# Side work planned by the engines that its next steps use, and the first two weight groups loaded and split in parts, in a two-layer decoder step on one core

## The chip, the cores and the metric

One core of a Trainium2 chip runs the whole step. The metric is the device time of one execution in microseconds (us). Shown before the change are three runs: a median of 1090.82 us, from 1090.24 to 1092.0.

## What is computed

Two decoder layers over 288 token columns: a prompt of 256 tokens and 8 sequences of 4 new tokens, with D = 1024. Cut to what matters:

```python
g, u_pool, u_conf, u_sc, q, k, v, qi, ki, wi = split_cols(x @ w_in)
a = pool_mixer(u_pool)                       # windows of 2, 4, 8, 16
b = silu(layer_norm(dwconv31(ga * sigmoid(gb)) + conv_b))
c = sb * dwconv3(sc_ * sh)
d = attend(q, k, v, topk(index_scores(qi, ki, wi)))
merged = sum(sigmoid(g[i]) * (branch[i] @ w_br[i]) for i in range(4))
x1 = layer_norm(ALPHA * x + merged @ w_o)
r = ALPHA * x1 + (silu(x1 @ w_hg) * (x1 @ w_hu)) @ w_ffn_out
r = r + (pe @ w_pe) * sigmoid(r @ w_pg)
y = layer_norm(r)
```

## The kernel before

All activations lie feature-major: 128 features on the partitions, 288 token columns. Every weight matrix is cut into 128 x 128 tiles, and the host lays the 2448 tiles out in the order in which TensorE will use them, in 306 groups of G = 8. Each product is made from three fp32r matmuls on numbers split into a high and a low part: high weight by high input, high weight by low input, low weight by high input. One group therefore holds 24 matmuls.

A weight group passes through three engines before TensorE can use it. SyncE's queue loads it (`wraw`, 512 KB, L239), ScalarE makes the high part (`whi`, L245), and VectorE subtracts it from the raw weights to make the low part (`wlo`, L252). `fetch` (L231 to 254) does this ahead of use: when TensorE comes to group g, the load of group g + 5, the high part of g + 3 and the low part of g + 2 are issued. `W` (called for each tile) calls `fetch` and then `side` when a new group begins.

`side` (L200) sets the order of everything that isn't a big product: it is a planner that runs while the program is written. The side jobs are Python generators (`conv`, `pool`, `sconv`, `topk` within the indexers, the two attentions). Each step of a job issues a few instructions and yields their estimated cost as a pair, (VectorE us, ScalarE us). Each group begins one tick, in which each engine gets a budget (1.96 us of VectorE, 2.3 us of ScalarE); the tick takes steps only while **both** engines have budget left:

```python
        while min(self.left) > 0:
            ready = [t for t in self.tasks if t.wake <= self.tick]
            if not ready:
                break
            ready = [t for t in ready if not t.low] or ready
```

A step that yields a plain number sleeps that many ticks. `conv`, the causal depthwise convolution with 31 taps (62 VectorE instructions at L653 and L655 for the prompt columns, six more from L661 for the samples, then a LayerNorm, a SiLU and `parts`, which splits the result at L633 and L637), is the only job of low priority. Where the main program needs a job's result, `finish` runs what is left of it on the spot, with no big product between its steps. `layer` calls `finish(conv)` after the products of the attention branch and before those of the convolution branch (`w_br_conv`), whose inputs are what L633 and L637 write. In the order before the change, `conv` is not done at that point in either layer: 8 calls of its generator are left in the first, 3 in the second.

The program begins in `run`: three warming matmuls on zeros (L1209), the input x in five loads (chunks 0, 1, 2-3, 4-5, 6-7 of 8), the weight groups between them, group 0 in two halves. Six column tiles are then accumulated over the 8 chunks of x by `outer` (L293, L295, L297), 18 matmuls for each chunk, called part 0 to part 7 here. Part k needs chunk k of x, cast and subtracted on VectorE (L1220, L1221), and the weight tiles 6k to 6k + 5; group 0 covers part 0 and two tiles of part 1.

Of the kernel before, what the change touches and what calls it, by code (L numbers as in the profile page):

```python
# [105 lines left out]

class Task:
    def __init__(self, gen, low):
        self.gen, self.wake, self.done, self.low = gen, 0, False, low


class Builder:
# [74 lines left out]
    def step(self, t):  # L187
# [6 lines left out]
        if isinstance(r, int):  # L194
            t.wake = self.tick + r
        else:
            self.left[0] -= r[0]
            self.left[1] -= r[1]

    def side(self):  # L200
# [3 lines left out]
        while min(self.left) > 0:  # L204
            ready = [t for t in self.tasks if t.wake <= self.tick]
# [25 lines left out]
    def fetch(self, g, only=0):  # L231
# [4 lines left out]
        while self.ndma <= to[0]:  # L236
            t = self.wp.tile([128, G * 128], F32, name="wraw", tag="wraw", bufs=4)
            for c in cut(self.ndma):
                nc.sync.dma_start(t[:, c], self.d["w"][self.ndma][:, c])  # L239
            self.raw[self.ndma] = t  # L240
            self.ndma += 1
        while self.nhi <= to[1]:
            t = self.wp.tile([128, G * 128], F32R, name="whi", tag="whi", bufs=4)
            for c in cut(self.nhi):
                nc.scalar.activation(t[:, c], self.raw[self.nhi][:, c], AF.Copy)  # L245
            self.hi[self.nhi] = t
            self.nhi += 1
        while self.nlo <= to[2]:
            t = self.wp.tile([128, G * 128], F32R, name="wlo", tag="wlo", bufs=3)
            raw = self.raw.pop(self.nlo)  # L250
            for c in cut(self.nlo):
                nc.vector.tensor_tensor(t[:, c], raw[:, c], self.hi[self.nlo][:, c].bitcast(F32), op=OP.subtract)  # L252
            self.lo[self.nlo] = t
# [28 lines left out]
    def outer(self, name, cols, rh, rl, nk):  # L282
        outs = []

        def part(k):
# [3 lines left out]
            while n < len(cols):  # L289
                now = min(G - len(self.keys) % G, len(cols) - n) if k < nk - 1 else 1  # L290
# [3 lines left out]
                for o, wh, wl in w:  # L294
                    m(o, wl, rh[:, k], start=False, stop=False)  # L295
                for o, wh, wl in w:
                    m(o, wh, rl[:, k], start=False, stop=k == nk - 1)  # L297
# [279 lines left out]
    def pool(self):  # L577
        nc, pe = self.nc, self.pe
        s1 = yield from self.get_b([128, 2, PE_])
# [16 lines left out]
        for c in range(2):  # L596
            for r0, src in ((0, s1), (64, s2)):
# [10 lines left out]
                yield 0.65, 0  # L608
        self.free(3)
# [764 lines left out]
```

## Time and profile before

| what | value |
|---|---|
| median of 3 runs | 1090.82 us |
| the profiled execution, its own time | 1090.84 us |
| its span, first to last instruction | 1089.1 us |
| TensorE busy (matmul) | 1066.8 us, 98% |
| VectorE busy | 770.1 us, 71% |
| ScalarE busy | 560.7 us, 51% |
| GpSimd busy | 171.6 us, 16% |
| DMA, mean | 173 GB/s |
| mean granted TensorE clock | 0.994 |

The busy time of TensorE is a sum of modelled matmul spans that overlap, so it isn't read as the share of useful work. How many matmuls begin in a stretch says more: a group of 24 takes about 3.2 us when nothing holds it up. A row of the timeline gives the start, the length, the engine, the line, the tile written and the tiles read, and in brackets how long the engine had been idle and what ended that.

### The profile page before, as it was taken

What the parts mean: (1) busy time and instruction counts of PE and PEld (TensorE: products, weight loads), DVE (VectorE), ACT (ScalarE), POOL (GpSimd) and SP (SyncE); (2) the same over time, 40 slices, a digit from 0 to 9 for tenths busy, and PEclk for the clock granted to TensorE, in tenths of its full rate; (3) what the DMA queues carried; (4) which work ended last, traced back from release to release, by engine and by line L of the source; (5) the groups of instructions that cost most, each with busy time, mean ns of one, the idle gap of its engine ahead of it and who ended that gap; (6) DMA issues with size and microseconds to landing.
All of it is one profiled execution on the core that took longest, in us unless ns stands there. A gap on an engine that the chain in (4) does not pass through costs nothing.

```text
span 1089.1 us, 20628 instructions
## 1 busy us (share of the span) xinstructions
PE 1066.8 (98%) x8138; PEld 1030.1 (95%) x8138; DVE 770.1 (71%) x1302; ACT 560.7 (51%) x930; POOL 171.6 (16%) x175
## 2 busy tenths in 40 slices
PE   8999999999999999999999999999989999999996
PEld 7999989899999999999999999998989999999995
DVE  5896958579885565544789877776697856655456
ACT  4875445445564444433579564644535644444334
POOL 0730002004510000000527100030045000000004
PEclk9999999999999999999999999999989999999998
DMA  8576556644445455555445854565433654554541
GB/s 302 164 244 212 173 174 232 195 147 135 155 148 184 155 173 168 166 170 167 154 154 171 295 171 155 195 213 184 140 132 117 193 174 156 167 170 166 175 136 44
DMA packets 61299, 188.57 MB, mean 173 GB/s; under 512 B 7538, under 2 KB 11666, under 8 KB 61202
## 3 DMA queue, kind: packets, MB, share of 16 engines
q1 hardware_dynamic: 60210, 183.69, 51.7%
q0 software_dynamic: 992, 3.57, 0.9%
q8 instruction: 64, 1.05, 0.4%
q14 instruction: 33, 0.27, 0.1%
HBM read 182.48 MB, written 4.75 MB: 172 GB/s over the span
## 4 chain that ended last, share of the span: by engine, by line
PE 89%; DVE 5%; issue 2%; ACT 2%; POOL 2%; DMA 1%; SPq 0%; DVEq 0%; POOLq 0%
PE mm L271 24%; PE mm L272 24%; PE mm L273 23%; PE mm L295 2%; PE mm L297 2%; PE mm L293 2%; DVE wlo L252 2%; PE ax L272 1%; PE ax L273 1%; PE ax L271 1%; POOL b L317 1%; PE ax L295 1%; PE ax L297 1%; POOL b L348 1%; PE ax L953 1%
## 5 line engine op out<-in xcount | busy, mean ns | idle before, releaser
L252 DVE TENSOR_TENSOR wlo<-wraw,whi 128x1024 fp32r<-128x1024 f32 (+1 forms) x307 | 383.3, 1251 | 155.0 <-issue 83.8
L271 PE MATMUL mm<-xh,whi 128*128 128x288 f32 x1536 | 455.1, 296 | 0.0
L273 PE MATMUL mm<-xh,wlo 128*128 128x288 f32 x1536 | 453.1, 295 | 0.3 <-DVE wlo L252 0.3
L272 PE MATMUL mm<-xl,whi 128*128 128x288 f32 x1536 | 453.2, 295 | 0.0
L245 ACT ACTIVATE whi<-wraw 128x1024 fp32r<-128x1024 f32 (+1 forms) x307 | 322.6, 1052 | 148.1 <-PE mm L272 74.0
L271 PEld LDWEIGHTS mm<-xh,whi 128*128 128x128 f32 x1536 | 288.8, 188 | 8.1 <-issue 6.4
L273 PEld LDWEIGHTS mm<-xh,wlo 128*128 128x128 f32 x1536 | 288.6, 188 | 0.9 <-DVE wlo L252 0.9
L272 PEld LDWEIGHTS mm<-xl,whi 128*128 128x128 f32 x1536 | 288.8, 188 | 0.3
L271 PE MATMUL mm<-b,whi 128*128 128x288 f32 x576 | 171.0, 297 | 0.3 <-DVE s L1030 0.2
L272 PE MATMUL mm<-b,whi 128*128 128x288 f32 x576 | 169.9, 295 | 0.0
L273 PE MATMUL mm<-b,wlo 128*128 128x288 f32 x576 | 169.7, 295 | 0.0
L271 PEld LDWEIGHTS mm<-b,whi 128*128 128x128 f32 x576 | 108.3, 188 | 1.3 <-issue 0.4
L272 PEld LDWEIGHTS mm<-b,whi 128*128 128x128 f32 x576 | 108.3, 188 | 0.3
L273 PEld LDWEIGHTS mm<-b,wlo 128*128 128x128 f32 x576 | 108.2, 188 | 0.0
L1031 POOL TENSOR_TENSOR m<-m,s 128x288 f32<-128x288 f32 x32 | 35.3, 1129 | 274.6 <-DVE s L1030 274.6
L315 POOL TENSOR_TENSOR b<-xf 128x288 f32<-128x288 f32 x4 | 4.9, 1218 | 442.4 <-DVE xf L1176 433.5
L1149 ACT ACTIVATE b<-s 128x288 fp32r<-128x288 f32 x44 | 19.3, 446 | 92.4 <-DVE s L1144 92.4
L655 DVE SCALAR_TENSOR_TENSOR b<-b,prm 128x256 f32<-128x256 f32 x120 | 62.1, 569 | 0.0
L1144 DVE TENSOR_TENSOR s<-s,mm 128x288 f32<-128x288 f32 x40 | 18.0, 454 | 50.5 <-PE mm L273 50.5
L1015 ACT ACTIVATE g<-mm 128x288 f32<-128x288 f32 x32 | 13.2, 412 | 67.7 <-PE mm L273 67.7
L1015 ACT ACTIVATE xf<-mm 128x288 f32<-128x288 f32 x32 | 13.2, 411 | 51.1 <-PE mm L273 51.0
L1152 DVE TENSOR_TENSOR b<-s,b 128x288 fp32r<-128x288 f32 x44 | 19.8, 458 | 19.5 <-ACT b L1149 19.5
(254 smaller groups left out, 1243.7 us busy)
## 6 DMA issues: line engine op xcount, KB each, us to landing
wraw<-in_w_dram SPq DMA_DIRECT2D x305, 512.0 KB, 3.5
kv<-in_ck_dram SPq DMA_DIRECT2D x32, 256.0 KB, 5.0
kv<-in_cv_dram SPq DMA_DIRECT2D x32, 256.0 KB, 4.3
out_ko_dram<-b POOLq DMA_DIRECT2D x2, 576.0 KB, 4.7
out_vo_dram<-b POOLq DMA_DIRECT2D x2, 576.0 KB, 6.9
kv<-in_kidx_dram SPq DMA_DIRECT2D x32, 32.0 KB, 3.0
xf<-in_x_dram SPq DMA_DIRECT2D x3, 288.0 KB, 6.5
b<-in_p_dram SPq DMA_DIRECT2D x3, 288.0 KB, 4.0
```

The lines of the kernel that those rows point to most:

```text
L245: nc.scalar.activation(t[:, c], self.raw[self.nhi][:, c], AF.Copy)
L252: nc.vector.tensor_tensor(t[:, c], raw[:, c], self.hi[self.nlo][:, c].bitcast(F32), op=OP.subtract)
L271: m(out, wh, rh, start=first, stop=False)
L272: m(out, wh, rl, start=False, stop=False)
L273: m(out, wl, rh, start=False, stop=last)
L293: m(o, wh, rh[:, k], start=k == 0, stop=False)
L295: m(o, wl, rh[:, k], start=False, stop=False)
L297: m(o, wh, rl[:, k], start=False, stop=k == nk - 1)
L655: nc.vector.scalar_tensor_tensor(o, e, wj, o, op0=OP.mult, op1=OP.add)
L1015: self.nc.scalar.activation(g, a, AF.Sigmoid)
L1031: nc.gpsimd.tensor_tensor(self.m[:, j], self.m[:, j], t, op=OP.add)
L1152: nc.vector.tensor_tensor(h[:, 1, i % 2], t, h[:, 0, i % 2].bitcast(F32), op=OP.subtract)
```

## The change

**The planner.** A task says which engines its next steps use (`needs`): both, which is the default, or VectorE alone. A step may be taken when every engine it needs has budget left, so a task that needs VectorE alone goes on after ScalarE's budget of the tick is spent. `conv` (taps and samples), `pool` (window sums) and `topk` declare such stretches with `yield VECTOR` and end them with `yield BOTH`.

**The first weights.** Group 0 is loaded and split in three parts (2, 2 and 4 tiles), group 1 in two (4 and 4); `outer` takes tiles by these parts (`room`). For the first two groups the second batch of matmuls is the one on the low input and the third the one on the low weight; it was the other way round. Chunk 0 of x is loaded from ScalarE's queue, chunks 2 and 3 are loaded apart, and the loads, splits and products are written out in the order of use. The warming matmuls read a constant that GpSimd sets and no longer one that VectorE sets.

```diff
+VECTOR, BOTH = (0,), (0, 1)
...
+        elif r is VECTOR or r is BOTH:
+            t.needs = r
...
-        while min(self.left) > 0:
-            ready = [t for t in self.tasks if t.wake <= self.tick]
+        can = lambda t: not t.done and t.wake <= self.tick and all(self.left[i] > 0 for i in t.needs)
+        while True:
+            ready = [t for t in self.tasks if can(t)]
             if not ready:
                 break
             ready = [t for t in ready if not t.low] or ready
             for t in ready:
-                if not t.done and min(self.left) > 0:
+                if can(t):
                     self.step(t)
...
+    def load(self, i):
+        g, c = self.ndma, cut(self.ndma)
+        if i == 0:
+            self.raw[g] = self.wp.tile([128, G * 128], F32, name="wraw", tag="wraw", bufs=4)
+        self.nc.sync.dma_start(self.raw[g][:, c[i]], self.d["w"][g][:, c[i]])
+        self.ndma += i == len(c) - 1
...
-                now = min(G - len(self.keys) % G, len(cols) - n) if k < nk - 1 else 1
+                now = min(room(len(self.keys)), len(cols) - n) if k < nk - 1 else 1
+                early = len(self.keys) < 2 * G
...
+                for second in ((1, 0) if early else (0, 1)):
+                    for o, wh, wl in w:
+                        if second:
+                            m(o, wh, rl[:, k], start=False, stop=not early and k == nk - 1)
+                        else:
+                            m(o, wl, rh[:, k], start=False, stop=False)
...
         bias = self.par("conv_b")
         es = [ce[:, c, 30 + TP:].rearrange("p (b w) -> p b w", b=NB) for c in range(2)]
+        yield VECTOR
         for j in range(31):
...
             yield 0.1, 0
+        yield BOTH
         self.free()
...
-        zero = self.s()
-        nc.vector.memset(zero, 0.0)
+        zero = nc.const_aps.tensor(0.0, (128, N), F32)
...
+        ks = [slice(0, 1), slice(1, 2), slice(2, 3), slice(3, 4), slice(4, 6), slice(6, 8)]
+        move(ks[0], nc.scalar)
+        for i in range(3):
+            self.load(i)
+        move(ks[1], nc.sync)
+        self.load(0)
+        move(ks[2], nc.sync)
+        self.load(1)
+        self.load(0)
+        move(ks[3], nc.sync)
+        move(ks[4], nc.sync)
+        self.load(0)
+        move(ks[5], nc.sync)
...
+        parts(ks[0])
+        for i in range(3):
+            self.high(i)
+            if i == 2:
+                parts(ks[1])
+            self.low(i)
+        part(0)
+        self.high(0)
+        self.low(0)
+        part(1)
...
+EDGES = {0: (0, 2, 4, 8), 1: (0, 4, 8)}
...
+def room(n):
+
+    g, i = divmod(n, G)
+    return next(e for e in EDGES.get(g, (0, G)) if e > i) - i
```

`high(i)` and `low(i)` are made like `load(i)`: they issue the ScalarE copy and the VectorE subtraction of part i of the next group. `move` is a load of x from the queue named, `parts` the cast and the subtraction of a chunk of x.

VectorE, second layer, before the change, from the convolution's centring (L677) to the first product of its branch (L1104). L252 is the low part of one weight group, so one such row stands for one group; L304 splits the next layer input `p`, L691 to L706 are the convolution's LayerNorm and SiLU, L637 its split, L1030 the gating of the attention branch:

```order
L677 SCALAR_TENSOR_TENSOR b<-ax,b 128x288 x2
L252 TENSOR_TENSOR wlo<-wraw,whi 128x1024
L304 TENSOR_TENSOR b<-b 128x576
L252 TENSOR_TENSOR wlo<-wraw,whi 128x1024
L691 RECIPROCAL s<-s 128x288
...
L696 TENSOR_TENSOR b<-b,s 128x288 x2
...
L706 TENSOR_TENSOR b<-b,s 128x288 x2
L1030 TENSOR_TENSOR s<-mm,g 128x288 x2
L637 TENSOR_TENSOR b<-b 128x288 x2
L252 TENSOR_TENSOR wlo<-wraw,whi 128x1024
L1104 TENSOR_TENSOR ax<-ax,xf 128x288
```

The same place with the change (L705 was L677, L271 was L252, L719 to L734 were L691 to L706, L328 was L304, L663 was L637, L1060 was L1030, L1134 was L1104):

```order
L705 SCALAR_TENSOR_TENSOR b<-ax,b 128x288 x2
L271 TENSOR_TENSOR wlo<-wraw,whi 128x1024 x2
L719 RECIPROCAL s<-s 128x288
L271 TENSOR_TENSOR wlo<-wraw,whi 128x1024
L724 TENSOR_TENSOR b<-b,s 128x288 x2
L727 TENSOR_SCALAR b<-b,prm 128x288 x2
L328 TENSOR_TENSOR b<-b 128x576
L271 TENSOR_TENSOR wlo<-wraw,whi 128x1024
L734 TENSOR_TENSOR b<-b,s 128x288 x2
...
L663 TENSOR_TENSOR b<-b 128x288 x2
...
L1134 TENSOR_TENSOR ax<-ax,xf 128x288
```

Before, the reciprocal and all that follows it stand behind L304, and one group's row lies between the last split L637 and the branch's first product. With the change the reciprocal, both scalings and both affine steps stand ahead of L328, only L734 and L663 behind it, and three groups' rows lie between L663 and L1134. The first layer is moved in the same way.

TensorE at the start of the program, before (parts 0 and 1; x2, x4 are equal instructions in a row):

```order
L1209 MATMUL ax<-s 128x288 x3
L293 MATMUL mm<-xh,whi 128x288 x4
L293 MATMUL ax<-xh,whi 128x288 x2
L295 MATMUL mm<-xh,wlo 128x288 x4
L295 MATMUL ax<-xh,wlo 128x288 x2
L297 MATMUL mm<-xl,whi 128x288 x4
L297 MATMUL ax<-xl,whi 128x288 x2
L293 MATMUL mm<-xh,whi 128x288 x2
L295 MATMUL mm<-xh,wlo 128x288 x2
L297 MATMUL mm<-xl,whi 128x288 x2
```

and with the change (L315 was L293, L321 was L295, L319 was L297):

```order
L1238 MATMUL ax<-const-float32-0.0 128x288 x3
L315 MATMUL mm<-xh,whi 128x288 x2
L319 MATMUL mm<-xl,whi 128x288 x2
L321 MATMUL mm<-xh,wlo 128x288 x2
L315 MATMUL mm<-xh,whi 128x288 x2
L319 MATMUL mm<-xl,whi 128x288 x2
L321 MATMUL mm<-xh,wlo 128x288 x2
L315 MATMUL ax<-xh,whi 128x288 x2
L319 MATMUL ax<-xl,whi 128x288 x2
L321 MATMUL ax<-xh,wlo 128x288 x2
```

Part 0 now runs in three pieces of six matmuls, each on its own piece of weights, and within a piece the low weight comes last.

## Rows read from the trace of the kernel before

**Rows 1.** The page, busy us (share of the span) and instructions of each engine.
```profile
PE 1066.8 (98%) x8138; PEld 1030.1 (95%) x8138; DVE 770.1 (71%) x1302; ACT 560.7 (51%) x930; POOL 171.6 (16%) x175
```

**Rows 2.** Waits of TensorE: us in total, times, longest, whole span.
```profile
PE ax L271 <- ACT b L633: 3.1, 1, 3.1
PE mm L293 <- ACT whi L245: 1.9, 2, 1.1
PE ax L272 <- DVE b L637: 1.3, 2, 0.8
```

**Rows 3.** Stretches: length, busy us (xinstructions) by engine; clock, DMA share, GB/s.
```profile
255.00:268.00 13.00, 11.83 (x83) 10.93 (x83) 12.48 (x22) 7.21 (x14) 7.07 (x8) 1.00 0.44 145
780.00:810.00 30.00, 25.87 (x174) 24.88 (x173) 27.08 (x42) 12.77 (x19) 13.74 (x14) 0.89 0.34 114
793.50:803.00 9.50, 5.54 (x22) 4.76 (x21) 8.99 (x14) 3.31 (x7) 5.77 (x6) 0.64 0.45 152
320.00:340.00 20.00, 20.00 (x154) 20.00 (x153) 13.42 (x22) 9.41 (x15) 0.00 (x0) 1.00 0.51 167
```

**Rows 4.** Timeline of the start: start us, us, engine, line, tiles [idle before].
```profile
0.76 0.40 SPq L1212 DMA_DIRECT2D xf<-in_x_dram  x1
...
1.21 0.89 SPq L239 DMA_DIRECT2D wraw<-in_w_dram  x2
...
1.24 3.17 PE L1209 MATMUL ax<-s 128*128 128x288 f32 x6 [1.24 <-DVE s L1206]
...
3.01 0.31 DVE L1220 CAST xh<-xf 128x288 fp32r<-128x288 f32 x1 [1.82 <-DMA xf<-in_x_dram]
...
3.35 0.46 DVE L1221 TENSOR_TENSOR xl<-xf,xh 128x288 fp32r<-128x288 f32 x1
...
4.54 0.63 ACT L245 ACTIVATE whi<-wraw 128x512 fp32r<-128x512 f32 x1 [2.50 <-DMA wraw<-in_w_dram]
...
5.20 0.69 DVE L252 TENSOR_TENSOR wlo<-wraw,whi 128x512 fp32r<-128x512 f32 x1 [1.39 <-ACT whi L245]
...
5.22 0.80 PE L293 MATMUL mm<-xh,whi 128*128 128x288 f32 x4 [0.81 <-ACT whi L245]
5.76 0.63 ACT L245 ACTIVATE whi<-wraw 128x512 fp32r<-128x512 f32 x1 [0.59 <-DMA wraw<-in_w_dram]
...
9.39 1.06 ACT L245 ACTIVATE whi<-wraw 128x1024 fp32r<-128x1024 f32 x1 [3.00 <-DMA wraw<-in_w_dram]
10.48 1.23 DVE L252 TENSOR_TENSOR wlo<-wraw,whi 128x1024 fp32r<-128x1024 f32 x1 [1.36 <-ACT whi L245]
...
11.43 1.06 ACT L245 ACTIVATE whi<-wraw 128x1024 fp32r<-128x1024 f32 x1 [0.98 <-DMA wraw<-in_w_dram]
...
17.70 0.69 PE L293 MATMUL mm<-xh,whi 128*128 128x288 f32 x4
```

**Rows 5.** Timeline where the second layer's convolution branch begins.
```profile
781.48 0.68 ACT L303 ACTIVATE b<-b 128x576 fp32r<-128x576 f32 x1
...
782.19 0.76 DVE L304 TENSOR_TENSOR b<-b 128x576 fp32r<-128x576 f32 x1 [4.28 <-ACT b L303]
...
796.46 0.81 ACT L633 ACTIVATE b<-b 128x288 fp32r<-128x288 f32 x2 [1.90 <-DVE b L706]
...
796.96 0.61 PE L271 MATMUL ax<-b,whi 128*128 128x288 f32 x1 [3.12 <-ACT b L633]
...
798.41 0.61 PE L272 MATMUL ax<-b,whi 128*128 128x288 f32 x1 [0.84 <-DVE b L637]
```

**Rows 6.** Two stretches, every engine (columns as in rows 3).
```profile
40.00:60.00 20.00, 19.74 (x150) 19.03 (x150) 19.86 (x28) 19.22 (x38) 14.78 (x12) 1.00 0.54 176
200.00:220.00 20.00, 20.00 (x170) 17.46 (x170) 10.76 (x19) 11.74 (x20) 0.00 (x0) 1.00 0.44 148
```

**Rows 7.** The same two, VectorE's taps of L655 alone.
```profile
40.00:60.00 20.00, 7.89 (x8) 1.00 0.54 176
200.00:220.00 20.00, 4.60 (x11) 1.00 0.44 148
```

More of the change, by code (lines that the diff above doesn't have):

```diff
@@ L104 @@
 NWARM = 3
+VECTOR, BOTH = (0,), (0, 1)
 class Task:
     def __init__(self, gen, low):
-        self.gen, self.wake, self.done, self.low = gen, 0, False, low
+        self.gen, self.wake, self.done, self.low, self.needs = gen, 0, False, low, BOTH
 class Builder:
@@ L236, in fetch, with high, low @@
         while self.ndma <= to[0]:
[L237 to L241, printed above, removed]
-        while self.nhi <= to[1]:
[L243 to L247, printed above, removed]
-        while self.nlo <= to[2]:
[L249 to L253, printed above, removed]
+            for i in range(len(cut(self.ndma))):
+                self.load(i)
+        while self.nhi <= to[1]:
+            for i in range(len(cut(self.nhi))):
+                self.high(i)
+        while self.nlo <= to[2]:
+            for i in range(len(cut(self.nlo))):
+                self.low(i)
[5 more added lines that the diff above has]
+        self.ndma += i == len(c) - 1
+    def high(self, i):
+        g, c = self.nhi, cut(self.nhi)
+        if i == 0:
+            self.hi[g] = self.wp.tile([128, G * 128], F32R, name="whi", tag="whi", bufs=4)
+        self.nc.scalar.activation(self.hi[g][:, c[i]], self.raw[g][:, c[i]], AF.Copy)
+        self.nhi += i == len(c) - 1
+    def low(self, i):
+        g, c = self.nlo, cut(self.nlo)
+        if i == 0:
+            self.lo[g] = self.wp.tile([128, G * 128], F32R, name="wlo", tag="wlo", bufs=3)
+        self.nc.vector.tensor_tensor(self.lo[g][:, c[i]], self.raw[g][:, c[i]], self.hi[g][:, c[i]].bitcast(F32),
+                                     op=OP.subtract)
+        if i == len(c) - 1:
+            self.raw.pop(g)
             self.nlo += 1
@@ L667, in conv @@
             yield 0.1, 0
+        yield BOTH
         self.free()
@@ L1209, in run, with move, parts @@
             nc.tensor.matmul(warm, zero[:, :128], zero, start=True, stop=True)
-        ks = [slice(0, 1), slice(1, 2), slice(2, 4), slice(4, 6), slice(6, 8)]
-        for i, k in enumerate(ks):
-            nc.sync.dma_start(self.xf[:, k], d["x"][:, k])
-            if i != 1:
-                self.fetch(max(i - 1, 0) - self.AHEAD_DMA, 1)
+        def move(k, queue):
+            queue.dma_start(self.xf[:, k], d["x"][:, k])
+        def parts(k):
+            nc.vector.tensor_copy(self.xh[:, k], self.xf[:, k])
+            nc.vector.tensor_tensor(self.xl[:, k], self.xf[:, k], self.xh[:, k].bitcast(F32), op=OP.subtract)
+        ks = [slice(0, 1), slice(1, 2), slice(2, 3), slice(3, 4), slice(4, 6), slice(6, 8)]
+        move(ks[0], nc.scalar)
+        for i in range(3):
+            self.load(i)
+        move(ks[1], nc.sync)
[7 more added lines that the diff above has]
+        move(ks[5], nc.sync)
         outs, part = self.conf_start(0)
         self.hold = True
-        for i, k in enumerate(ks):
-            if i != 1:
-                self.fetch(max(i - 1, 0) - self.AHEAD_HI, 2)
-            nc.vector.tensor_copy(self.xh[:, k], self.xf[:, k])
-            nc.vector.tensor_tensor(self.xl[:, k], self.xf[:, k], self.xh[:, k].bitcast(F32), op=OP.subtract)
-            if i != 1:
-                self.fetch(max(i - 1, 0) - self.AHEAD_LO, 3)
-            for j in ((0,), (), (1,), (2, 3), ())[i]:
-                part(j)
+        parts(ks[0])
+        for i in range(3):
+            self.high(i)
+            if i == 2:
+                parts(ks[1])
+            self.low(i)
+        part(0)
+        self.high(0)
+        self.low(0)
+        part(1)
+        self.high(1)
+        parts(ks[2])
+        self.low(1)
+        self.high(0)
+        self.low(0)
+        part(2)
+        parts(ks[3])
+        part(3)
+        parts(ks[4])
+        self.high(0)
+        self.low(0)
+        parts(ks[5])
         self.hold = False
```

11 lines of the change are left out of this document (5 added, 6 removed).

## The prediction

> **What bounds the kernel now.** I read the page first. TensorE is busy 98% of the span and no other engine passes 71% [rows 1], so time can only come from moments in which TensorE has nothing to start. The busy share hides these, since modelled matmul spans overlap; I therefore took stretches of 20 us over the whole span and counted matmuls. An undisturbed one starts 154 in 20 us [rows 3], 0.130 us each, and one weight group of 24 takes 3.1 us. Most stretches are like that. The large exceptions are three, and the waits of TensorE name two of them: matmuls that wait for the convolution's split (L633 on ScalarE 3.1 us, L637 on VectorE 1.3 us in two places), and at the start for the high weights (1.9 us in two places) [rows 2].
>
> - *Second layer, around 795 us.* 780 to 810 us hold 174 matmuls, which need 174 x 0.130 = 22.6 us of the 30: 7.4 us are lost [rows 3]. The timeline shows 3.12 us idle until L633 and 0.84 us until L637 [rows 5]. The rest is the clock: 793.5 to 803 us hold 22 matmuls at a mean granted clock of 0.64, between full (2.4 GHz) and half (1.2 GHz) [rows 3], where 9.5 us would hold 73 undisturbed.
> - *First layer, around 260 us.* 255 to 268 us hold 83 matmuls, 10.8 of 13 us: 2.2 us lost, at full clock [rows 3].
> - *The start.* Part 0 starts at 5.22 us and part 4 at 17.70 us [rows 4]. The 72 matmuls between need 72 x 0.130 = 9.4 us and take 12.5.
>
> **The change, part by part.** The sum is made against the profiled execution's own 1090.84 us, which is the median of the runs (1090.82) within 0.02. No matmul is added or removed, the same weights are copied and subtracted, two fewer ScalarE table loads stand in the program; I cost those at nothing, since ScalarE is busy 51% [rows 1] and no large wait names them.
>
> *The convolution.* Why was it late? On VectorE, L304 (the split of the next input) waits for ScalarE's L303, which stands behind the last gate, and that waits for TensorE: VectorE sits idle for 4.28 us and gets on at 782.95 us [rows 5]. All of the LayerNorm and SiLU, from the reciprocal on, is queued behind it, with four groups' low weights and the gating of the attention branch between, and the last split is not done when TensorE arrives. With the change the reciprocal, scaling and affine steps stand ahead of that split, only four convolution instructions behind it, and in both layers the planner is done with the convolution three groups (9.4 us of TensorE) before its branch, so `finish` has nothing left to run. Can those four still be late? Behind 782.95 us stand two low-weight rows (1.23 us each [rows 4]), a pair L734 (1.41 us for L706, its old name [rows 5]), a gating pair and a pair L663 (bounded by L734's): together some 6.5 us, done near 789.5 us, while the branch began to wait at 793.8 us (796.96 less 3.12). So 4 us are to spare. I take 6.9 of the 7.4 us in the second layer and 1.8 of the 2.2 us in the first, leaving 0.5 and 0.4 for short waits in the same window whose cause is the gating. Lower ends: in the second layer 4.0 us (3.12 + 0.84, if the clock's cost came back elsewhere), in the first 0.5 us (the smaller wait of L637, 1.3 less 0.8 [rows 2]). The clock goes along with the wait: it fell after TensorE had stood still, and with no such stop I see nothing to lower it.
>
> *The start.* Take the landing times of before against the KB that had been asked for up to then: 144 KB at 3.0 us, 400 at 4.5, 656 at 5.8, 1600 at 9.4, 2400 at 11.4 (the idle time before each ends with the DMA) [rows 4]. In the new order x0 and the first 128 KB piece make 272 KB: 3.8 us by interpolation; the second piece 400 KB, 4.5; the third 656, 5.8; x1 6.3; group 1's halves 7.3 and 8.8, x2 between at 7.9; group 2 10.3. Copies: 1.06 us for 1024 columns and 0.63 for 512 give 0.42 for 256; subtractions 1.23, 0.69 and so 0.42. Then the first matmul starts at 3.8 + 0.42 = 4.2 us, about when the warming ends (1.24 + 3.17 = 4.4, which can start somewhat earlier without VectorE's zeros) [rows 4]. Piece 3's high part is ready at 6.4, its low part at 7.8 (VectorE does chunk 1 first, 6.3 + 0.77); part 0 ends at 8.0. Part 1's first six matmuls end at 8.8, its other twelve run on group 1's first half, split by 8.6, to 10.4; part 2's first twelve to 12.0 on the second half. Group 2 is copied by 11.4 and subtracted by 12.6, so part 2 ends at 12.9 and part 3, 18 matmuls of 0.130, at 15.3. Part 4 starts at 15.3 instead of 17.7: **2.4 us**. Chunks 4-5 and group 3 arrive by 12.7 at the same rate and are split by 15.8, before their low part is due. Upper end: no stall at all from 4.2 on, 4.2 + 9.4 = 13.6, so 4.1 us. Lower end: 0, all of it waiting for group 2. I take the walk's 2.4, since each of its durations is a row's or halves one.
>
> *What the planner's denser ticks may cost.* Jobs that need VectorE alone now run in ticks whose ScalarE budget is spent, so VectorE is fuller between 40 and 200 us and at the same places of the second layer. A tick's 1.96 us and a low-weight row of 1.23 make 3.2 us, about a group's time, and the low weights are asked for two groups ahead, so a lag below some 4 us costs nothing. Pool in the second layer now ends one group before its branch and not two. The page loads of the second half of the sequences come closer together in the first layer and farther apart in the second, past which SyncE's queue must still bring a group every 3.1 us. For such new waits, bounded by 0 and by about the 2.2 us that the first layer's convolution cost, I take **0.3 us**.
>
> Sum: 2.4 + 1.8 + 6.9 - 0.3 = 10.8 us, so 1080.0 us. All best ends give 1077.1, all worst 0 + 0.5 + 4.0 - 2.2 = 2.3, 1088.5.
>
> **The rivals.**
> *The cut pieces give nothing* (12%). The bytes before group 2 is whole are nearly the same and every DMA has its own landing; if pieces cost in landings what they save in waiting, part 4 starts at 17.7 as before and the time is 1082.4. For it: the two 256 KB halves, issued together at 1.21 us, were waited for until 4.54 and 5.76 us, so a small DMA is not quickly there. Against it: the second half came 1.22 us after the first, while the first group of 512 KB came 3.6 us later with x between [rows 4]. The Trainium skill speaks for it ("DMA: Bandwidth & Descriptors", Measured): it says to batch loads to 1 MiB or more, and its table (0.95 us at 64 KB, 6.15 at 1 MB) gives an estimate of 1.3, 2.0 and 3.4 us for 128, 256 and 512 KB if they ran one by one. By that, five pieces take 8.6 us and the old two halves and a whole 7.4, and the start would gain 1.2 us instead of 2.4. The rows' 1.22 us for 256 KB is below the page's 2.0.
>
> *The wait moves and stays in part* (10%). L328 still blocks VectorE until the last gate, and four instructions of the convolution are behind it. If VectorE arrives there late, half of 8.7 us stays: 1084.4. It decides once those four are more than 4 us later than I put them.
>
> *VectorE becomes the bound, and it is slower* (4%). A tap (L655) takes 7.89 / 8 = 0.99 us between 40 and 60 us, where GpSimd is busy 14.8 of 20 us, and 4.60 / 11 = 0.42 us between 200 and 220 us, where GpSimd is idle [rows 6, 7]; its estimate in the planner is 0.49. In the first stretch VectorE is busy 19.86 of 20 us and TensorE starts 150 matmuls, not 154 [rows 6]. Were the taps that move earlier to meet GpSimd, a tick of four would take 1.23 + 4 x 0.99 = 5.2 us against 3.1. From seven such ticks on (7 x 2.1 us less the 4 us of lag allowed) the whole gain is eaten; with ten, 17 us are lost and the time is 1090.84 - 10.8 + 17 = 1097. Against it: by the order most of the moved taps come to groups 33 to 56, of which 200 to 220 us is a part, and there GpSimd did nothing [rows 6].
>
> **How the numbers follow.** The forecast has 74%: 1080.0 us, on its own 1077 to 1083. The two middle rivals lie at 1082.4 and 1084.4. The range 1077.0 to 1084.5 takes in the best ends and both, and leaves out the slower rival and my own chance of having the walk wrong. About 0.2% (2.2 us) is what a measurement of this kernel tells from no change. All but the last rival gain 6 us or more: faster 0.94, same 0.02, slower 0.04.
>
> **What would show it.** In the changed profile: the first real matmul near 4.2 us and part 4 near 15.3; no wait of TensorE for the convolution's two split lines; some 225 matmuls instead of 174 in the 30 us around the second layer's branch, at a clock of 1.00. If waits for the low weights between groups 28 and 60 grow past a microsecond, the third rival holds; if the first matmul is early and part 4 still at 17.7, the first.

## The result

Over the runs the changed kernel takes 1084.12 us (median of 4, 1083.62 to 1084.61), the one before 1090.72 us on the same chip (median of 4, 1090.24 to 1092.0): a ratio of 0.993 with a 95% interval of 0.9918 to 0.9942. That is 6.6 us faster; the forecast was 1080.0 us, in a range from 1077.0 to 1084.5. The profiled execution of the changed kernel took 1083.62 us, with a span of 1081.8 us, 7.3 us less than the span before.

The page's busy line of the changed kernel answers to [rows 1], and TensorE is still what the time goes by:

```profile
PE 1066.2 (99%) x8138; PEld 1030.5 (95%) x8138; DVE 770.9 (71%) x1305; ACT 557.5 (52%) x930; POOL 174.4 (16%) x175
```

The longest waits of TensorE (us in total, times, longest) answer to [rows 2]. The convolution's two split lines (L659 and L663 now) are gone from them, and two waits stand there which before were smaller or not there: low weights of groups 8 and 10 (L294 waits for L271), and a bank that VectorE's gating of a branch (L1060) frees late:

```profile
PE ax L424 <- DVE q L419: 1.0, 1, 1.0
PE mm L294 <- DVE wlo L271: 0.8, 2, 0.4
PE mm L292 <- DVE s L1060: 0.8, 2, 0.6
```

Two stretches around the convolution branches answer to [rows 3] (length, busy us by engine, clock, DMA share, GB/s). Where the first layer had 83 matmuls in 13 us it has 100; the second has 224 in 30 us where it had 174, and its mean clock is 1.00 and not 0.89:

```profile
252.00:265.00 13.00, 13.00 (x100) 13.00 (x99) 11.00 (x19) 5.84 (x10) 9.48 (x9) 1.00 0.51 163
778.50:808.50 30.00, 29.79 (x224) 29.56 (x224) 27.73 (x48) 14.14 (x23) 16.59 (x16) 1.00 0.48 159
```

The start answers to [rows 4]. The first rows are x's first chunk, TensorE's first real matmul, its one later wait, of 0.71 us (the third piece's low weights), and part 4:

```profile
3.55 0.31 DVE L1243 CAST xh<-xf 128x288 fp32r<-128x288 f32 x1 [3.55 <-DMA xf<-in_x_dram]
...
4.20 0.85 PE L315 MATMUL mm<-xh,whi 128*128 128x288 f32 x2 [0.20 <-ACT whi L264]
...
7.99 0.53 PE L321 MATMUL ax<-xh,wlo 128*128 128x288 f32 x2 [0.71 <-DVE wlo L271]
...
15.50 0.69 PE L315 MATMUL mm<-xh,whi 128*128 128x288 f32 x4
```

And the timeline where the second layer's convolution is finished answers to [rows 5]. VectorE still waits for L327, but 1.49 us and not 4.28; the last split L663 is done at 787.05 us, and the only wait of TensorE near there is 0.21 us, behind it:

```profile
780.01 0.68 ACT L327 ACTIVATE b<-b 128x576 fp32r<-128x576 f32 x1
...
780.72 0.76 DVE L328 TENSOR_TENSOR b<-b 128x576 fp32r<-128x576 f32 x1 [1.49 <-ACT b L327]
781.40 1.22 DVE L271 TENSOR_TENSOR wlo<-wraw,whi 128x1024 fp32r<-128x1024 f32 x1
782.53 0.82 DVE L734 TENSOR_TENSOR b<-b,s 128x288 f32<-128x288 f32 x2
784.00 1.69 DVE L271 TENSOR_TENSOR wlo<-wraw,whi 128x1024 fp32r<-128x1024 f32 x1
785.62 1.43 DVE L663 TENSOR_TENSOR b<-b 128x288 fp32r<-128x288 f32 x2
...
795.87 0.79 PE L315 MATMUL mm<-b,whi 128*128 128x288 f32 x4 [0.21 <-ACT b L1138]
```

**Where the 7.3 us come from.** A weight group has 24 matmuls, so counting weight matmuls in the two traces gives the time at which each group starts. The lead of each kernel over the one before (us, profiled executions; the first line is when the group starts in the kernel before):

```
start of group        3     12     68     70    122    148    220    223    276    300    end
before, us         17.7   47.9  260.0  268.3  437.9  520.4  790.4  806.9  979.7 1055.9
changed kernel    +2.20  +1.36  +0.97  +2.92  +2.80  +2.23  +1.33  +7.73  +7.68  +7.10  +7.31
planner alone     +0.35  -0.22  -0.41  +1.57  +1.47  +1.47  +0.79  +7.13  +7.15  +7.15  +7.08
start alone       +2.14  -0.55  -0.61  -0.61  -0.63  -1.20  -1.27  -1.22  -1.25  -1.82  -1.61
b moved           +2.42  +0.48  +0.30  +2.28  +2.30  +2.29  +0.96  +7.28  +7.46  +7.44  +7.66
key first         +2.22  +2.75  +2.59  +4.57  +4.48  +4.47  +3.64  +9.97 +10.02 +10.00 +10.22
key, old start    -0.14  +0.39  +0.59  +2.57  +2.62  +2.62  +1.89  +8.23  +8.23  +8.23  +7.61
conv only         +2.31  +1.26  +0.01  +1.96  +1.81  +1.24  -0.78  +5.62  +5.79  +5.22  +5.42
```

The changed kernel's line reads: the start gains 2.20 and loses 0.84 of it by 48 us; the first layer's side work costs 0.39, its convolution brings 1.95 (groups 68 to 70); 0.57 go between groups 122 and 148, the second layer's side work costs 0.90, its convolution brings 6.40 (220 to 223), and another 0.58 go between groups 276 and 300. Two of these losses are where nothing waits: both stretches are the stage of `w_ffn_out`. The same 60 us of that stage, in the kernel before and then in the changed one:

```profile
440.00:500.00 60.00, 60.00 (x456) 60.00 (x455) 29.22 (x33) 22.98 (x26) 0.00 (x0) 1.00 0.52 168
```
```profile
440.00:500.00 60.00, 60.00 (x452) 60.00 (x451) 28.90 (x32) 22.64 (x26) 0.00 (x0) 1.00 0.51 166
```

TensorE is busy throughout at full clock in both, and starts four matmuls fewer: in the trace one every 133.3 ns instead of 132.2, over 22 groups in each layer.

### The profile page after: what moved, and what is told of

Its sections match the earlier page's. It is cut to its first block, busy times and chain, and to the rows that moved or that the text cites. A ratio compares the mean times of both kernels' runs of the same rounds, so it can differ in the third digit from the quotient of the medians.

```text
span 1081.8 us, 20642 instructions
## 1 busy us (share of the span) xinstructions
PE 1066.2 (99%) x8138; PEld 1030.5 (95%) x8138; DVE 770.9 (71%) x1305; ACT 557.5 (52%) x930; POOL 174.4 (16%) x175
## 4 chain that ended last, share of the span: by engine, by line
PE 91%; DVE 4%; ACT 2%; POOL 2%; issue 1%; DMA 0%; SPq 0%; DVEq 0%; POOLq 0%; ACTq 0%
PE mm L292 24%; PE mm L293 24%; PE mm L294 24%; PE mm L319 2%; PE mm L321 2%; PE mm L315 2%; DVE wlo L271 1%; PE ax L293 1%; PE ax L292 1%; PE ax L294 1%; PE ax L321 1%; POOL b L341 1%; PE ax L319 1%; PE ax L315 1%; POOL b L372 1%
## 5 line engine op out<-in xcount | busy, mean ns | idle before, releaser
L271 DVE TENSOR_TENSOR wlo<-wraw,whi 128x1024 fp32r<-128x1024 f32 (+1 forms) x309 | 384.4, 1246 | 144.6 <-issue 79.6
L294 PE MATMUL mm<-xh,wlo 128*128 128x288 f32 x1536 | 453.1, 295 | 0.9 <-DVE wlo L271 0.8
L293 PE MATMUL mm<-xl,whi 128*128 128x288 f32 x1536 | 453.2, 295 | 0.0
L294 PEld LDWEIGHTS mm<-xh,wlo 128*128 128x128 f32 x1536 | 288.6, 188 | 1.7 <-DVE wlo L271 1.6
L293 PEld LDWEIGHTS mm<-xl,whi 128*128 128x128 f32 x1536 | 288.8, 188 | 0.4
L293 PE MATMUL mm<-b,whi 128*128 128x288 f32 x576 | 169.9, 295 | 0.0
L294 PE MATMUL mm<-b,wlo 128*128 128x288 f32 x576 | 169.5, 294 | 0.0
L294 PEld LDWEIGHTS mm<-b,wlo 128*128 128x128 f32 x576 | 108.5, 188 | 0.0
L293 PEld LDWEIGHTS mm<-b,whi 128*128 128x128 f32 x576 | 108.1, 188 | 0.3
L1061 POOL TENSOR_TENSOR m<-m,s 128x288 f32<-128x288 f32 x32 | 38.2, 1226 | 273.5 <-DVE s L1060 273.5
```

Of the source, the lines that this page charges most:

```text
L271: self.nc.vector.tensor_tensor(self.lo[g][:, c[i]], self.raw[g][:, c[i]], self.hi[g][:, c[i]].bitcast(F32), op=OP.subtract)
L293: m(out, wh, rl, start=False, stop=False)
L294: m(out, wl, rh, start=False, stop=last)
L1061: nc.gpsimd.tensor_tensor(self.m[:, j], self.m[:, j], t, op=OP.add)
```

## The experiments

The runs were made on several chips. A ratio is to the kernel before on the same chip, whose median was 1091.68 us beside the runs named `e1`, 1091.98 beside `e2`, 1091.55 beside `e3` and 1091.44 beside `e4`; a difference of 1 us between medians of two such groups is therefore read only together with the traces.

**The two parts apart.** `e1_planner_alone` has the planner's hunks on the old start; `e1_start_alone` has the new start, with the yields taken out:

```diff
-        yield VECTOR
...
-        yield BOTH
```

> Only the planner's part of the change (Task.needs, the loop in side and the yields in conv, pool and topk); the start is that of before. If the parts add up: 1.9 us from the first layer's convolution and 6.7 us from the second's, less about 1 us for new short waits among the moved side work, so 1083.0 to 1083.6 us; part 4 at 17.7 us. On the stage of w_ffn_out (matmuls start every 133.33 ns in the changed kernel, every 132.23 ns before, about 1.1 us in both layers): theory A, the cadence follows where the b tiles lie in SBUF; here the b tiles start at byte 114176, as before, so 132.2 ns is expected. Rival B, it follows the order of the side work or the rotation of the b slots, which here is that of the changed kernel: 133.3 ns, and 1084.2 us or more.

> Only the start's part of the change; the yields of VECTOR and BOTH are taken out, so the planner is that of before. Theory: first real matmul at 4.2 us, part 4 at 15.5 us, 2.2 us ahead of before; in the stretch from 27 to 60 us, where VectorE is busy 19.86 of 20 us before too, about 0.8 us of it is given back; the convolution's waits stay as before. By theory A (place of the b tiles, which start at byte 103232 here as in the changed kernel) w_ffn_out runs at 133.3 ns and costs 1.1 us: in all a gain of only 0.3 us, 1090.4 us. By rival B (order of the side work) w_ffn_out stays at 132.2 ns: 1089.3 us. If nothing of the start is given back, each of the two is 0.8 us less.

Measured: the planner alone 1083.94 us against 1091.68 before (ratio 0.9926, 0.9915 to 0.9938), the start alone 1091.70 us (0.9999, 0.999 to 1.0009). So by time the planner's part is the whole gain, as far as the intervals tell, and no gain of the start by itself is seen; the 0.3 us that theory A had left it lie inside its interval too. The table shows why: its 2.14 us are there at group 3 and gone, with 0.55 more, at group 12. In that kernel TensorE stops for 2.02 us for the low weights of group 8:

```profile
34.17 0.40 PE L294 MATMUL mm<-xh,wlo 128*128 128x288 f32 x1 [2.02 <-DVE wlo L271]
```

The `w_ffn_out` stage ran at 132.2 ns with the planner alone and at 133.3 ns with the start alone: theory A's side, not B's.

**The place of the tiles in SBUF.** The old start took its zeros from an `s` tile, which made the `s` tiles the first to be laid out; without it the `b` tiles come first and start at byte 103232 and not 114176 (read from the two built programs). Modulo 128 that is 64 and not 0. `e1_b_aligned` moves the `b` tiles and what is laid out behind them by 64 bytes, `e1_all_aligned` the weight tiles too (the matmuls of `w_ffn_out` read `b` and weight tiles alone):

```diff
-        self.prm_next = self.sb.tile([128, NPAR], F32, name="prm", tag="prm", bufs=2)
+        self.prm_next = self.sb.tile([128, NPAR + 12], F32, name="prm", tag="prm", bufs=2)[:, :NPAR]
```
```diff
         self.xl = self.cst.tile([128, KD, N], F32R, name="xl")
+        self.cst.tile([128, 16], F32, name="shift")
```

> The changed kernel with 12 unused columns more in each of the two parameter tiles, so that the b tiles start at byte 103296 (807 x 128) and not 103232 (806.5 x 128); no instruction changes its kind or its place. Theory A, in the sharper form that what counts is whether a matmul's moving tile starts on a multiple of 128 bytes: w_ffn_out at 132.2 ns again, 1.1 us faster than the changed kernel, 1083.0 us. Rival B (order of the side work or rotation of the slots): 133.3 ns and no difference.

> The changed kernel with an unused tile of 64 bytes behind xl, which moves the weight tiles (whi from byte 71616 = 559.5 x 128 to 71680 = 560 x 128, wlo and wraw likewise) and everything behind them by 64 bytes, the b tiles with them to 103296. Theory A: at least the 1.1 us of w_ffn_out, so 1083.0 us. If the place of the stationary tiles counts too, the 132.2 ns of all the other stages become shorter: each 0.1 ns less would be 0.7 us over 7344 matmuls. If only the moving tile counts, all stages run at 132.2 ns, and the time is that of the kernel in which only the b tiles are moved, within 0.3 us.

Measured: 1083.38 us (ratio 0.9919, 0.9906 to 0.9933) and 1088.43 us (0.9967, 0.9956 to 0.9979). Moving the `b` tiles gives back the 456 matmuls; this is too little for the intervals of the times to show (the changed kernel's overlaps), but the lead over groups 122 to 148 stays at 2.30 where the changed kernel lost 0.57. Moving the weights onto a multiple of 128 as well made everything worse, against each of my expectations: now an ordinary stage, 320 to 380 us, has 452 matmuls too, where the kernel before has 456. The two stretches with only `b` moved, and then with all moved:

```profile
320.00:380.00 60.00, 60.00 (x456) 60.00 (x455) 36.86 (x50) 27.60 (x41) 0.00 (x0) 1.00 0.52 162
440.00:500.00 60.00, 60.00 (x456) 60.00 (x455) 29.39 (x33) 23.13 (x26) 0.00 (x0) 1.00 0.52 169
```
```profile
320.00:380.00 60.00, 60.00 (x452) 60.00 (x452) 36.46 (x52) 26.96 (x41) 0.00 (x0) 1.00 0.53 162
440.00:500.00 60.00, 60.00 (x452) 60.00 (x452) 29.25 (x33) 22.86 (x26) 0.00 (x0) 1.00 0.52 167
```

So the moving tile's own place doesn't decide it; the place of the weights counts too. `e2_shift32` tried a third distance, with weights at 96, `b` at 64 and `xh`, `xl` at 0:

```diff
         self.xl = self.cst.tile([128, KD, N], F32R, name="xl")
+        self.cst.tile([128, 8], F32, name="shift")
+        self.sb.tile([128, 8], F32, name="shift2", tag="shift2", bufs=1)
...
-        self.prm_next = self.sb.tile([128, NPAR], F32, name="prm", tag="prm", bufs=2)
+        self.prm_next = self.sb.tile([128, NPAR + 12], F32, name="prm", tag="prm", bufs=2)[:, :NPAR]
```

> The changed kernel with unused bytes in SBUF so that, modulo 128 bytes, the weight tiles start at 96, the b tiles at 64, xh and xl at 0 as ever. So far: moving tile and weights at 0 and 64: 132.2 ns; 64 and 64, or 0 and 0: 133.3 ns. Theory A1, it costs when both lie in the same half of 128 bytes: w_ffn_out (64 and 96) 133.3 ns, the other stages (0 and 96) 132.2 ns, 1084.1 us. Theory A2, it costs only when both offsets are equal: 132.2 ns in all stages, 1083.0 us. If the distance itself counts, in steps of 32 bytes, a stage may lie below 132.2 or between the two: each 0.1 ns is 0.6 us over the stages outside w_ffn_out.

Measured: 1088.94 us (0.9972, 0.9962 to 0.9982), with 448 matmuls in 60 us against `xh` and 456 against `b`:

```profile
320.00:380.00 60.00, 60.00 (x448) 60.00 (x448) 36.37 (x53) 26.95 (x41) 0.00 (x0) 1.00 0.55 165
440.00:500.00 60.00, 60.00 (x456) 60.00 (x455) 29.34 (x35) 22.81 (x28) 0.00 (x0) 1.00 0.53 171
```

Both sharper theories fall: A1, since 96 and 64 lie in the same half and run at 132.3 ns, and A2, since 96 and 0 differ and run slowest, at 134.5 ns. What holds is the table: weights and moving tile at 64 and 0, 132.2 ns; 96 and 64, 132.3 ns; 64 and 64, or 0 and 0, 133.3 ns; 96 and 0, 134.5 ns. With the weights at 64 a moving tile at 64 is 1.1 ns slower than one at 0, with the weights at 96 it is 2.2 ns faster: it is the pair that counts, and neither place by itself. Why is open.

**Where the start's gain goes.** ScalarE's timeline in the changed kernel, from the copy of group 8's high weights on: behind it two gates (L537) with their table load, then eight copies of the index queries' rotation (L477 and L478; two of them shown), and only then the next high copy:

```profile
23.68 1.06 ACT L264 ACTIVATE whi<-wraw 128x1024 fp32r<-128x1024 f32 x1 [2.66 <-PE mm L319]
24.76 1.28 ACT L537 ACT_TABLE_LOAD   x1
26.05 0.71 ACT L537 ACTIVATE s<-mm 128x288 f32<-128x288 f32 x2
26.79 0.40 ACT L477 ACTIVATE s<-ax 32x288 f32<-32x288 f32 x1
27.20 0.40 ACT L478 ACTIVATE s<-ax 32x288 f32<-32x288 f32 x1
...
30.13 1.06 ACT L264 ACTIVATE whi<-wraw 128x1024 fp32r<-128x1024 f32 x1
```

VectorE multiplies the rotation (L479) at 30.14 us, and group 8's low weights, queued behind that, come at 30.51; TensorE wants them at 31.82 and gets them at 32.26:

```profile
30.14 0.46 DVE L479 TENSOR_TENSOR qi<-ax,const 128x288 f32<-128x288 f32 x1 [1.21 <-ACT s L478]
30.51 1.69 DVE L271 TENSOR_TENSOR wlo<-wraw,whi 128x1024 fp32r<-128x1024 f32 x1
```
```profile
32.26 0.40 PE L294 MATMUL mm<-xh,wlo 128*128 128x288 f32 x1 [0.44 <-DVE wlo L271]
```

From the high copy to TensorE's start these are 8.6 us, and they are the same 8.6 us with `b` moved and with the start alone. What differs is when the chain begins. In every trace here the copy starts 0.1 us after group 8's weights have landed (also in the changed kernel, where the row names a matmul). The same copy in the kernel before, and then with the start alone:

```profile
25.01 1.06 ACT L245 ACTIVATE whi<-wraw 128x1024 fp32r<-128x1024 f32 x1 [2.39 <-DMA wraw<-in_w_dram]
```
```profile
25.61 1.06 ACT L264 ACTIVATE whi<-wraw 128x1024 fp32r<-128x1024 f32 x1 [3.63 <-DMA wraw<-in_w_dram]
```

So against the kernel before the chain begins 1.33 us earlier in the changed kernel (23.68), 0.43 earlier with `b` moved (24.58) and 0.60 later with the start alone, while TensorE comes to group 8 between 1.9 and 2.4 us earlier in all three. The leads at group 9 follow the chain and not TensorE: 1.52, 0.62 and -0.40 us. The rest, 0.2 us in each, is the room that the kernel before had: its low weights of group 8 are ready at 33.55 us and are used at 33.88, without a wait:

```profile
31.85 1.70 DVE L252 TENSOR_TENSOR wlo<-wraw,whi 128x1024 fp32r<-128x1024 f32 x1
```
```profile
33.88 0.30 PE L273 MATMUL mm<-xh,wlo 128*128 128x288 f32 x1
```

Why the weights land when they do, and not 2.2 us earlier with everything else, no run here shows. `e2_ki_first` (with the `b` tiles moved) takes the rotation out of the chain in the first layer:

```diff
-        for i in range(2):
-            self.rope(qi[:, i], qs[i], 128)
+        ropes = lambda: [self.rope(qi[:, i], qs[i], 128) for i in range(2)]
+        if l:
+            ropes()
+        else:
+            self.cost(2.0, 2.6)
         a, = self.proj("w_in", [C_KI], *x, bank=self.ax)
+        if l == 0:
+            ropes()
+            self.cost(-2.0, -2.6)
```

> The kernel with the b tiles on a multiple of 128 bytes, and in the first layer the rotation of the two index queries (rope) is written behind the index key's projection, so that group 9's high copy stands ahead of the eight rotation copies on ScalarE and group 8's low weights ahead of L479 on VectorE; the planner's costs are counted where they were. Theory C: the 2.2 us that the start gains are given back at 32 to 34 us because group 8's low weights stand behind two SiLU gates with their table load and eight rotation copies (a chain of 8.6 us that starts with group 8's high copy, whenever the start lets TensorE arrive). Then the low weights are ready near 28.7 us, the wait of 0.7 to 2.3 us at 32 to 34 us is gone, group 9 starts 1.2 to 2.2 us ahead of the kernel before (there 0.7), and the time is 1082.0 us, 1.4 us below the kernel with the b tiles moved alone. Rival D: VectorE's full stretch from 40 to 60 us, or the landing of the weights, takes it back a few groups later: the lead at group 20 is the same 0.3 to 0.7 us and so is the time, 1083.4 us.

Measured: 1081.06 us (0.9905, 0.9888 to 0.9921). Group 8's low weights now follow the gates' products on VectorE, 2.7 us earlier:

```profile
27.69 0.18 DVE L547 TENSOR_TENSOR b<-mm,s 128x32 f32<-128x32 f32 x1
27.79 1.21 DVE L271 TENSOR_TENSOR wlo<-wraw,whi 128x1024 fp32r<-128x1024 f32 x1
```

No wait of TensorE is left between 25 and 60 us, and the lead is 2.75 at group 12 and 2.59 at group 68, where the kernel with `b` moved had 0.48 and 0.30. Theory C stands, with the landing as the beginning of its chain: the copy starts at 24.11 us here, and the low weights are ready 4.9 us later, at 29.0 us, where the changed kernel needs 8.5; TensorE comes to group 8 at 31.39 us. D, that VectorE's full stretch takes the gain back anyway, falls. `e3_ki_old_start` makes the same edit on the old start, and asks whether the start is worth its 2.2 us now:

> The planner's part of the change with the start of before, b tiles on a multiple of 128 bytes as there, and the index queries' rotation behind the index key's projection as in the kernel that reached 1081.1 us; this kernel differs from that one by the start alone. Theory C (what the start gained was taken back by the chain behind the gates, and stays once the chain is out of the way): this kernel is slower by the start's 2.2 us, 1083.2 us, and its group 20 starts 2.2 us later. Rival: moving the rotation gains by itself, whatever the start, and the start is worth only the 0.6 us that it was worth without it: 1081.6 us.

Measured: 1082.47 us (0.9913, 0.9898 to 0.9928), 1.4 us behind by the medians, and the intervals overlap, so the times alone don't decide between 1083.2 and 1081.6. The leads say more: 2.36 us apart at group 12, 2.00 at group 68, 1.74 at group 223 and 1.77 at group 300 (2.61 at the end, but 0.84 of that falls behind group 300). So the start's gain stays for the most part once the chain is gone, 1.7 to 2.4 us by the leads. The rival has a part of the truth: on the old start, too, the moved rotation gains 1.0 us by itself (from -0.41 to 0.59 at group 68, from 7.15 to 8.23 at group 300). Of its 2.3 us on the new start, therefore, only some 1.3 are the start's own gain let through.

**The cut pieces.** `e2_old_cut` keeps the new order of use, with the first group in two halves and the second whole:

```diff
-EDGES = {0: (0, 2, 4, 8), 1: (0, 4, 8)}
+EDGES = {0: (0, 4, 8)}
```

(the loads, copies and subtractions of the start are then called once for each remaining piece).

> The changed kernel with the first group in its two old halves and the second group whole, in the new order of use. If the cut pieces bring what the walk said: the first matmul at 5.2 instead of 4.2 us and part 4 near 16.4 instead of 15.5 us. By the first rival (pieces cost in landings what they save in waiting) part 4 stays at 15.5 us or comes earlier. The whole time is that of the changed kernel, 1084.1 us, within 0.4 us in both cases, since what the start gains is given back at 32 us.

Measured: first matmul at 5.04, part 4 at 16.58 us, and 1083.35 us in all (0.9921, 0.9906 to 0.9937); at the end of the kernel nothing of it can be told. That part 4 comes 1.1 us later fits the walk, but it doesn't show what the pieces bring. In this execution the 18 matmuls of part 0 waited for nothing and yet took 4.39 us, one every 0.24 us, and from part 1 on they came every 0.13 us, without a wait, up to part 4:

```profile
5.04 1.33 PE L315 MATMUL mm<-xh,whi 128*128 128x288 f32 x4 [1.03 <-DVE xl L1244]
...
9.43 0.42 PE L315 MATMUL mm<-xh,whi 128*128 128x288 f32 x2
...
16.58 0.69 PE L315 MATMUL mm<-xh,whi 128*128 128x288 f32 x4
```

One every 0.24 us is the pace at half the clock (in the kernel before, 800 to 803 us, granted clock 0.51). It held to 9.29 us here (where the record of the granted clock begins, at 1.00) and to 5.71 us in the changed kernel; the executions differ in this, and with the old start it ended at 4.20, 8.81 and 10.15 us in three of them. So the 1.1 us may be the clock's. An estimate from the same trace: at 0.132 us a matmul part 0 would end near 7.4 us, TensorE would wait for group 1's high part (ready at 8.94) and low part (10.20), and part 4 would start near 15.5 us, where the changed kernel has it. What the pieces bring is open: nothing by this estimate, 1.1 of the 2.2 us by the difference as it was measured.

`e4_low_first`, on the 1081.06 us kernel, puts the third piece's low weights ahead of x's chunk 1 on VectorE:

```diff
-            if i == 2:
-                parts(ks[1])
             self.low(i)
+        parts(ks[1])
```

> The kernel that reached 1081.1 us, with the third piece's low weights subtracted ahead of the split of x's chunk 1 on VectorE, which waits for the chunk's DMA until 6.5 us (the piece's high part is ready at 6.0). Walk: the low part is ready at 6.7 instead of 7.9 us, chunk 1 at 7.4 instead of 7.3, so the wait of 0.3 to 1.2 us near 7.9 us goes and part 4 starts near 15.0 instead of 15.5 us. Theory C with the chain out of the way: this stays to the end, 1080.6 us. Rival: group 2's landing takes it back, part 4 at 15.4 us or more and 1081.1 us.

Measured: 1081.08 us (0.9903, 0.9886 to 0.992). The wait near 7.9 us is gone, part 1 starts 0.9 us earlier, and another wait takes its place: group 2's weights arrive at 10.05 us, and TensorE waits for their low part. Part 4 starts at 15.43 us, not 15.0. The rival holds:

```profile
10.05 1.06 ACT L264 ACTIVATE whi<-wraw 128x1024 fp32r<-128x1024 f32 x1 [0.67 <-DMA wraw<-in_w_dram]
```
```profile
12.42 0.53 PE L321 MATMUL ax<-xh,wlo 128*128 128x288 f32 x2 [0.27 <-DVE wlo L271]
...
15.43 0.69 PE L315 MATMUL mm<-xh,whi 128*128 128x288 f32 x4
```

**Which jobs must be freed.** `e2_conv_only` is the changed kernel with the yields left in `conv` alone; `e3_no_topk` and `e3_no_pool` take them out of one job each, on the 1081.06 us kernel (the edit is that of `e1_start_alone`, in those functions only).

> The changed kernel without the yields of VECTOR and BOTH in pool and topk, so that only the convolution may run in ticks whose ScalarE budget is spent. Theory: the convolution is finished three groups before its branch in both layers as in the changed kernel, and all of its gain stays (1.9 and 6.7 us); the new wait of 0.9 us at 718 us (TensorE for VectorE's L1060, behind pool's last steps) is gone, since pool is finished two groups before its branch again. So 1083.2 us, some 0.9 us below the changed kernel. Rival: pool and topk are needed too, since what they vacate is what the convolution uses; then the convolution's splits are late again by 1 us or more and the time is 1085 us or above.

> The kernel that reached 1081.1 us with the yields of VECTOR and BOTH taken out of topk; conv and pool keep theirs. The kernel in which only the convolution had them lost 2.2 us between groups 175 and 213 and 0.9 us more in the first layer's side work, most of it in the sample attention's matmuls against the cache pages, waiting for a page's DMA and for VectorE. Theory E: that loss hangs on topk, which decides when index_sample ends (group 31 with the yields, 36 without) and so when the pages are asked for: 1083.1 us. Rival F: it hangs on pool's yields: 1081.1 us.

> The kernel that reached 1081.1 us with the yields of VECTOR and BOTH taken out of pool; conv and topk keep theirs. By theory E pool's yields bring nothing: the planner ends every task at the same group but pool in the first layer, one group earlier: 1081.1 us within 0.4 us, the wait of 0.6 us near 716 us (TensorE for VectorE's gating of the sconv branch) still there. By rival F it loses up to 2 us, 1083 us.

Measured: 1086.38 us for the convolution alone (0.9951, 0.9937 to 0.9965), 1083.10 us without topk's (0.9922, 0.9908 to 0.9935), 1081.65 us without pool's (0.9911, 0.9896 to 0.9926). In the first of the three my theory was wrong on the time and right on the convolution: it brings 1.95 and 6.40 us there too (table, conv only), and the loss is in the side work, 2.0 us between groups 148 and 220 and 1.3 between 12 and 68, where the changed kernel loses 0.9 and 0.4. Its TensorE waits in the second layer's side work, 560 to 790 us, show a cache page's DMA and the gating of the pool branch:

```profile
PE ax L979 <- DMA kv<-in_ck_dram: 0.7, 1, 0.7
PE mm L292 <- DVE m L1053: 0.7, 1, 0.7
```

Without topk's yields the same two waits appear at the same size, and 2.0 us are lost by the medians, as theory E said (3.7 us in the profiled executions, 2.0 of them between groups 12 and 68). Without pool's, 0.6 us are lost, with overlapping intervals: little or nothing. The 0.6 us wait for L1060 stays in that kernel, so pool's later end in the second layer is not what makes it; I have not found what does.

## Why the prediction was right, and 4.1 us too hopeful

The largest term came about by the mechanism that was told. That 1084.12 us lies inside the stated range is in part luck: the range ends at 1084.5 for the sake of the second rival (1084.4), whose mechanism did not come about, and the forecast's own 1077 to 1083 misses. In the terms of the sum, the profiled executions have 2.2 for the start, 1.95 and 6.4 for the convolution, 2.1 of new waits and 1.15 that were in no term: 7.3 us in place of 10.8. Another 0.7 is between these executions and the medians, since that of the changed kernel was the fastest of its four. The 0.130 us for a matmul is a little low: the 154 of a window take in those that began before it (151 start in it), and from start to start a matmul took 0.132 us; it changes no term by more than 0.1 us.

- *The convolution, 6.9 and 1.8 us*: right. Measured 6.40 and 1.95 (groups 220 to 223 and 68 to 70), and all of it with the planner alone too. The mechanism was the one told: L328 still waits, and the four instructions behind it were put at 789.5 us and are done at 787.05. The clock went along with the wait, as supposed: 1.00 in those 30 us, while the start alone, whose convolution is late as before, has the fall to 0.5 again, at 797 us.
- *The start, 2.4 us*: right as a walk and wrong as a term of the sum. First matmul at 4.20 us (4.2 forecast), part 4 at 15.50 (15.3). But the step "part 4 starts at 15.3 instead of 17.7: 2.4 us" carried a lead at 15 us to the end without asking what TensorE meets next. It met a chain that begins when group 8's weights land and goes through ScalarE, and that in the kernel before was done only 0.3 us ahead of need. By the medians the start is worth 0.6 us (1083.94 without it, 1083.38 with it and `b` in place, with runs that overlap), and 1.4 once the chain is gone, 1.7 to 2.4 by the leads.
- *New waits, 0.3 us*: the failed term. Its bound of 2.2 us was the right size in this trace: 0.84 by group 12, 0.39 in the first layer's side work and 0.90 in the second's make 2.1 (the first of the three is 1.94 with `b` moved, where the weights land later). I took the low end because a lag below 4 us "costs nothing" on VectorE. The wait by group 12 is no such lag: VectorE's subtraction stands behind the landing and ScalarE's rotation copies. What makes VectorE's gating L1060 late in the side work is open.
- *"No matmul is added or removed, the same weights are copied": cost nothing*. True of the count, not of the price. Removing one `s` tile at the start moved the `b` tiles by an odd multiple of 64 bytes against the weights, and 2 x 22 groups of matmuls ran 1.1 ns slower each: 0.57 and 0.58 us, in no term.
- *The rivals*: the first, as it was told (part 4 still at 17.7), falls, but what the pieces themselves bring to the 2.2 us is not shown. The Trainium skill ("DMA: Bandwidth & Descriptors", Measured) asks for batched loads; the estimate from its table, which was measured on loads that GpSimd issues and not SyncE, gave the start a gain of 1.2 us in place of 2.4, and the trace shows 2.2. The wait did not move behind L328. VectorE did not become the bound: no wait for low weights is left between 60 and 250 us, a tap costs 0.99 us beside GpSimd and 0.42 without it, as before [rows 7], and where 11 taps stood in 200 to 220 us there are 17 now, still without GpSimd beside them. In the first of these rows 7.02 us leave out the part of a tap pair that ran before 40 us; the four pairs take 1.90 to 2.02 us each:

```profile
40.00:60.00 20.00, 7.02 (x8) 1.00 0.53 174
200.00:220.00 20.00, 7.14 (x17) 1.00 0.42 141
```

## What to carry to other kernels

A gain at the start is worth what the next queue lets through: before adding it to a sum, follow the lead to the next place where an in-order engine has long work ahead of what TensorE needs, see what that work itself waits for and whether this moves with the start, and how much room the old kernel had. Here two lines of program order, rotation behind projection, turned 0.6 us into 1.4 or more, and with the `b` tiles in place they make 1081.06 us, 0.9905 of the kernel before, where the changed kernel is at 0.993; of all kernels here only `e4_low_first` is as fast. A start is also compared at the same clock: look at the pace of the first matmuls before a difference there is put down to an edit. And when an edit adds or drops a tile, compare the places of all tiles in the built programs, not only the instructions.

## What was not expected of the hardware

At full clock and with no wait, the start-to-start time of the same 128x288 matmul was 132.2 (132.3), 133.3 or 134.5 ns, depending on where its moving tile and its weight tile start modulo 128 bytes. Over a whole kernel that is a matter of 5 us (1083.38 and 1088.43 us for programs that differ by a shift of the weight tiles by 64 bytes). Five pairs of places were seen; no rule that covers them was found. The Trainium skill ("TensorE: Matmul & The Clock Gate", Step-by-step: what each phase is for) says that TensorE reads its moving operand and its weights through two independent ports, so that loading the next weights takes nothing from the running matmul; read that way, the places of the two tiles should not matter to each other, and here they do, by up to 2.3 ns in 132.2. Whether the ports have a part in it no run here shows.
